# The latent attention of a two-layer trunk: its steps put in a fixed order on three engines, weight conversions at named blocks, and one value tile earlier

## The chip, the cores and the metric

One Trainium2 chip, one of its cores. The time is the device time of one launch in microseconds (us); a kernel's time is the median of several runs. The engines are named PE (matrix products and transposes), DVE (vector), ACT (scalar and activation), POOL (GpSimd) and SP, whose queue issues the transfers from HBM. Each runs its own program in order and waits on semaphores for the others.

## The reference

Two layers of a decoder trunk, 512 positions of width 1024, one sequence, float32. Each layer is feed-forward, token mixer, feed-forward, all with a norm before and after and a modulation (shift, scale, gate) computed from a vector `c`. The mixer of the first layer, which alone is touched here, is latent attention with 16 heads; the second layer's is a dilated window attention.

```python
def mla(h, w_in, q_norm, w_q_up, kv_norm, w_kv_up, w_o):
    lat = h @ w_in
    cq, ckv = lat[..., :384], lat[..., 384:640]
    k_rope = lat[..., 640:][:, :, None, :]
    q = (rmsnorm(cq, q_norm) @ w_q_up).reshape(B, S, 16, 64 + 32)
    kv = (rmsnorm(ckv, kv_norm) @ w_kv_up).reshape(B, S, 16, 64 + 64)
    q = concat([q[..., :64], rope(q[..., 64:], pos)])
    k = concat([kv[..., :64], rope(k_rope, pos) broadcast to the heads])
    v = kv[..., 64:]
    s = q k^T * 96 ** -0.5, causal;  p = softmax(s)   # per head
    return (p v, heads side by side) @ w_o
```

## The kernel before

Six sub-layers run one after the other: feed-forward, latent attention, feed-forward, feed-forward, dilated attention, feed-forward. Every weight is split, after its transfer, into two numbers of a reduced format: `whi` (a rounded copy, on ACT, L132) and `wlo` (what the rounding left, on DVE, L134, in two halves). A product is then three matmuls on PE (L147 to L149). PE is the engine with most to do, and the rest of the program is written to keep it supplied.

Latent attention works feature-major: a tile is 128 features (partitions) by 512 positions. First the latents are projected and normed (`head`, `norm`). The norm's last step, per latent tile and half of the positions, is DVE L773, then a rounded copy on ACT L776 (`hh`), then the rest on DVE L777 (`hl`). Then `rest` takes over. It works on 8 pairs of heads, c = 0 to 7, and for each pair on four groups of 128 query positions, i = 0 to 3. One (c, i) is a block, n = 4c + i, 32 blocks in all. Causality makes the scores of block i 128(i + 1) wide. For each of the two heads of the pair, a block does

- score: one matmul (L879) into a bank of PSUM; on DVE a masked scale with a minimum over the row (L882, called the reduce here), which reads the bank and so sets it free; on ACT the exponential with its sum (L885); then, for both heads at once, a reciprocal on DVE (L888), and the division: head 0 on DVE (L890), head 1 on ACT (L891);
- turn: transposes of the probabilities on PE (L907) into banks of a second kind ("aux"), and copies to SBUF: for i < 2 on DVE (L909), for i of 2 and 3 one head on ACT (L911) and one on DVE (L912). The copies are named `silu` for even and `gg` for odd i;
- weigh: after odd i, the products of the probabilities with the values of blocks i - 1 and i (L928), into one aux bank for the whole pair; after i = 3 `put_o` splits that bank into two parts (ACT L708, DVE L709).

`Pipe(2)` staggers them: in the step that scores a block, PE also turns the block two steps back and weighs an earlier one. Banks: four for scores and projections ("mm", taken in turn), four of the kind "aux". A matmul into a bank waits until what the bank held was read.

Beside the blocks, a table `BESIDE` names for each block which projections are written right behind it: `key(g, p)` (copies on ACT L809, DVE L810, POOL L812), `query(g, p)` (two copies on ACT L819), `value(j, e)` (6 products and a copy on ACT L797), and `rope(g)`. `rope` makes the rotated part of four heads' queries from one product: a shuffle and a multiplication on DVE (L825, L826), one multiplication on POOL (L827), the addition on DVE (L828), then copies: two on ACT (L836), two on POOL (L834). Here g is a group of four heads; `weight(g, 0)` holds its key and rope columns and `weight(g, 1)` its query columns, and each is transferred and converted where it is first called.

Instructions of all engines are ordered by a scheduler, which sees the program in the order in which it is written and moves instructions by its own estimates. So in the kernel before, the order on PE, ACT and DVE in this stretch is the scheduler's. Conversions of the weights, for instance, stand between the steps of the blocks wherever the scheduler put them, one half apart from the other in places.

Of the kernel before, what the change touches and what calls it, by code (L numbers as in the profile page):

```python
# [535 lines left out]
class Ffn:  # L536
# [104 lines left out]

class Pipe:
# [71 lines left out]
class Mla(Mixer):  # L714
# [66 lines left out]
    def project(self, w, at, us):  # L781
# [3 lines left out]
            t.mm3(b, [x[:, at + j, :] for x in w], self.latn[u], j == 0, j == len(us) - 1)  # L785
        return b

    def value(self, j, e):
        t = self.t
        if not self.wv:  # L790
            self.wv += [t.weights(t.a["mla_v"][k], flat=True) for k in range(2)]
        b = t.bank()
        for k in range(2):
            ls = [x[:, j * P : (j + 1) * P] for x in self.latn[k]]
            t.mm3(b, ls, [x[:, e * SEQ : (e + 1) * SEQ] for x in self.wv[k]], k == 0, k == 1)
        self.v[j, e] = t.s()
        t.nc.scalar.activation(self.v[j, e], b, AF.Copy)  # L797
# [23 lines left out]
    def rope(self, g):  # L821
        t, nc = self.t, self.t.nc
        b = self.project(self.weight(g, 0), 4, (3, 4, 5))
        t1, t2 = t.s(), t.s()
        nc.vector.stream_shuffle(t2, b, [(c + 16) % 32 for c in range(32)])  # L825
        nc.vector.tensor_tensor(t1, b, self.cos, ALU.mult)  # L826
        nc.gpsimd.tensor_tensor(t2, t2, self.sin, ALU.mult)  # L827
        nc.vector.tensor_tensor(t1, t1, t2, ALU.add)  # L828
        for p in range(2):
            q = self.q[2 * g + p] = [t.s() for _ in range(2)]  # L830
            for e in range(2):
                r = t1[64 * p + 32 * e : 64 * p + 32 * e + 32]
                if p:
                    nc.gpsimd.tensor_scalar(q[e][64:96], r, 1.0, 0.0, ALU.mult, ALU.add)  # L834
                else:
                    nc.scalar.activation(q[e][64:96], r, AF.Copy)  # L836


    BESIDE = {
        1: (("query", 0, 1),),  # L840
        2: (("value", 3, 0),),
        3: (("key", 1, 0),),
        4: (("rope", 1),),
        5: (("query", 1, 0),),
        6: (("value", 0, 1),),
        8: (("key", 1, 1),),
        9: (("query", 1, 1),),
# [13 lines left out]
        28: (("part", 0),),  # L861
        29: (("part", 1),),
        30: (("part", 2),),
    }

    def attend(self, c, i, pipe):
        t, nc = self.t, self.t.nc
        sc = 96.0**-0.5
        if i == 0:
            self.st = t.tmp.tile([P, 4, 6], F32, tag="st", name="st", bufs=3), {}  # L870
        st, box = self.st
        q, k = self.q[c], self.k[c]

        def score(i):
            n = (i + 1) * P
            box[i] = []
            for e in range(2):
                s = t.bank()[:, :n]
                nc.tensor.matmul(s, q[e][0:96, i * P : n], k[e][0:96, :n], start=True, stop=True)  # L879
                p = (t.t("u", UB) if i % 2 else t.t("sq", SB))[:, :n]  # L880
                nm, z = st[:, i, e : e + 1], st[:, i, 2 + e : 3 + e]
                nc.vector.tensor_tensor_reduce(  # L882
                    p, s, self.mask[:, SEQ - n :], -sc, 3e38, ALU.add, ALU.min, accum_out=nm
                )
                nc.scalar.activation(p, p, AF.Exp, bias=nm, scale=-1.0, accum_out=z)  # L885
                box[i].append(p)
            r = st[:, i, 4:6]
            nc.vector.reciprocal(r, st[:, i, 2:4])  # L888
            p = box[i]
            nc.vector.tensor_scalar(p[0], p[0], r[:, 0:1], None, ALU.mult)  # L890
            nc.scalar.activation(p[1], p[1], AF.Copy, scale=r[:, 1:2])  # L891

        def turn(i):
            n = (i + 1) * P
            tag = "gg" if i % 2 else "silu"
            ps = [t.bank("aux")]
            ys = [t.t(tag)]
            if i < 2:
                ps.append(ps[0][:, n:])
                ys.append(ys[0][:, n:])  # L900
            else:
                ps.append(t.bank("aux"))
                ys.append(t.t(tag))
            for e in range(2):
                for j in range(i + 1):
                    r = slice(j * P, (j + 1) * P)
                    nc.tensor.transpose(ps[e][:, r], box[i][e][:, r], t.ident)  # L907
            if i < 2:
                nc.vector.tensor_copy(ys[0][:, : 2 * n], ps[0][:, : 2 * n])  # L909
            else:  # L910
                nc.scalar.activation(ys[0][:, :n], ps[0][:, :n], AF.Copy)  # L911
                nc.vector.tensor_copy(ys[1][:, :n], ps[1][:, :n])  # L912
            box[i] = ys

        def weigh(i):
            if i == 0:
                box["o"] = t.bank("aux")
            elif i % 2:
                for q in (i - 1, i):
                    products(q)  # L920
            if i == 3:
                self.put_o(box["o"])

# [12 lines left out]

        pipe.push(i, score, turn, weigh)

    def rest(self):
        self.t.gates(self)  # L940
        self.wv, self.wqk, self.v, self.q, self.k = [], {}, {}, {}, {}
        pipe = Pipe(2)
        self.key(0, 0)
        self.value(0, 0)
        self.value(1, 0)
        self.key(0, 1)
        self.t.count(99)
        self.rope(0)
        self.query(0, 0)
        self.value(2, 0)  # L950
        for c in range(8):
            for i in range(4):
                if (c, i) == (7, 0):
                    self.t.new_y()
                self.attend(c, i, pipe)
                for name, *args in self.BESIDE.get(4 * c + i, ()):
                    getattr(self, name)(*args)
        for ns in ((3, 4, 5), (6, 7)):
            pipe.step()
            for n in ns:  # L960
                self.part(n)
        pipe.flush()


class Dil(Mixer):
# [622 lines left out]
```

## Time and profile before

| | |
|---|---|
| median of 3 runs | 2256.52 us (2256.39 to 2257.5) |
| the profiled execution, its own time | 2258.68 us |
| its span, first to last instruction | 2256.5 us |
| mean granted clock of PE | 0.996 of full speed |
| busy: PE, DVE, ACT, POOL | 2217.8, 1183.6, 848.3, 106.3 us |
| latent attention's `rest` | about 436 to 590 us of the span |

Times in the profile count from the span's start. A row of the timeline gives start, length, engine, line, operation, what is written from what, shapes, a count where several are run together, and in brackets the idle time ahead with what ended it. A row of a group gives total busy time and the mean of one in ns, then the engine's idle time before these instructions with the releasers. A row of waits gives who waited for whom: total us, times, the longest.

### The profile page before, as it was taken

What the parts mean: (1) busy time and instruction counts of PE and PEld (TensorE: products, weight loads), DVE (VectorE), ACT (ScalarE), POOL (GpSimd) and SP (SyncE); (2) the same over time, 40 slices, a digit from 0 to 9 for tenths busy, and PEclk for the clock granted to TensorE, in tenths of its full rate; (3) what the DMA queues carried; (4) which work ended last, traced back from release to release, by engine and by line L of the source; (5) the groups of instructions that cost most, each with busy time, mean ns of one, the idle gap of its engine ahead of it and who ended that gap; (6) DMA issues with size and microseconds to landing.
All of it is one profiled execution on the core that took longest, in us unless ns stands there. A gap on an engine that the chain in (4) does not pass through costs nothing. (4 is left out here: it accounts for less than half of the span.)

```text
span 2256.5 us, 30151 instructions
## 1 busy us (share of the span) xinstructions
PE 2217.8 (98%) x11354; PEld 1868.9 (83%) x11354; DVE 1183.6 (52%) x2691; ACT 848.3 (38%) x1730; POOL 106.3 (5%) x143
## 2 busy tenths in 40 slices
PE   7999999999999999999999999999999998999998
PEld 5888888877898888898888889988899878888887
DVE  7666575677665356474464463234424466333344
ACT  4422234577633132352221353434342545322232
POOL 1000001210110000020000010000000002000000
PEclk9999999999999999999999999999999999999999
DMA  8575762311255365334653533334343442233231
GB/s 309 158 245 186 195 219 69 110 52 57 66 167 181 110 187 181 127 121 136 175 179 119 159 117 111 101 103 93 72 114 110 89 129 66 83 120 101 79 112 38
DMA packets 124056, 290.33 MB, mean 129 GB/s; under 512 B 44786, under 2 KB 49157, under 8 KB 123910
## 3 DMA queue, kind: packets, MB, share of 16 engines
q1 hardware_dynamic: 123910, 288.41, 41.6%
q8 instruction: 89, 1.46, 0.3%
q14 instruction: 57, 0.47, 0.1%
HBM read 281.76 MB, written 4.49 MB: 127 GB/s over the span
## 5 line engine op out<-in xcount | busy, mean ns | idle before, releaser
L134 DVE TENSOR_TENSOR wlo<-raw,whi 128x512 fp32r<-128x512 f32 (+1 forms) x714 | 467.4, 692 | 593.8 <-ACT whi L132 592.6
L147 PE MATMUL mm<-s,whi 128*128 128x512 f32 (+1 forms) x1932 | 722.1, 374 | 2.4 <-ACT whi L132 2.4
L149 PE MATMUL mm<-s,wlo 128*128 128x512 f32 (+1 forms) x1932 | 719.2, 372 | 0.0
L148 PE MATMUL mm<-s,whi 128*128 128x512 f32 (+1 forms) x1932 | 719.0, 372 | 0.0
L132 ACT ACTIVATE whi<-raw 128x1024 fp32r<-128x1024 f32 (+1 forms) x357 | 368.8, 1048 | 785.2 <-PE mm L148 531.6
L147 PEld LDWEIGHTS mm<-s,whi 128*128 128x128 f32 x1932 | 364.3, 189 | 69.3 <-issue 3.5
L149 PEld LDWEIGHTS mm<-s,wlo 128*128 128x128 f32 x1932 | 364.6, 189 | 63.5
L148 PEld LDWEIGHTS mm<-s,whi 128*128 128x128 f32 x1932 | 364.6, 189 | 61.7
L147 PE MATMUL mm<-whi,s 128*128 128x512 f32 (+1 forms) x1040 | 407.1, 391 | 4.1 <-ACT s L708 4.1
L149 PE MATMUL mm<-whi,s 128*128 128x512 f32 (+1 forms) x1040 | 404.7, 389 | 1.2 <-DVE s L709 1.2
L148 PE MATMUL mm<-wlo,s 128*128 128x512 f32 (+1 forms) x1040 | 405.2, 390 | 0.0
L147 PEld LDWEIGHTS mm<-whi,s 128*128 128x128 f32 x1040 | 211.2, 203 | 39.7 <-ACT s L708 4.5
L149 PEld LDWEIGHTS mm<-whi,s 128*128 128x128 f32 x1040 | 211.3, 203 | 36.1 <-DVE s L709 1.6
L148 PEld LDWEIGHTS mm<-wlo,s 128*128 128x128 f32 x1040 | 211.3, 203 | 34.0 <-issue 0.3
L169 DVE CUSTOM_DVE_ANT_0 raw<-raw,cs 128x1024 f32<-128x1024 f32 x130 | 159.4, 1232 | 124.4 <-DMA raw<-w_mod 123.9
L463 DVE TENSOR_TENSOR s<-mm,s 128x512 f32<-128x512 f32 x112 | 76.8, 690 | 121.1 <-PE mm L149 121.1
L322 POOL TENSOR_TENSOR mv<-mv,mhalf 128x1 f32<-128x1 f32 x48 | 36.2, 756 | 1493.5 <-DVE mv L321 1491.0
L1092 ACT ACTIVATE s<-mm 128x128 f32<-128x128 f32 (+3 forms) x109 | 33.1, 358 | 163.6 <-PE mm L149 159.7
L586 ACT ACTIVATE s<-gg 128x512 fp32r<-128x512 f32 (+1 forms) x97 | 57.4, 592 | 47.1 <-DVE gg L585 47.1
L585 DVE TENSOR_TENSOR gg<-silu,mm 128x512 f32<-128x512 f32 (+1 forms) x95 | 59.9, 630 | 12.0 <-ACT silu L583 12.0
L1203 ACT ACTIVATE u<-u,y 128x128 f32<-128x128 f32 x128 | 49.6, 397 | 23.8 <-issue 13.1
L583 ACT ACTIVATE silu<-mm 128x512 f32<-128x512 f32 (+1 forms) x95 | 51.4, 541 | 18.3 <-PE mm L149 18.2
(185 smaller groups left out, 1682.7 us busy)
## 6 DMA issues: line engine op xcount, KB each, us to landing
raw<-w_gu SPq DMA_DIRECT2D x168, 512.0 KB, 4.2
raw<-w_mod SPq DMA_DIRECT2D x130, 512.0 KB, 4.6
raw<-w_down SPq DMA_DIRECT2D x88, 512.0 KB, 4.3
raw<-dil_in SPq DMA_DIRECT2D x47, 512.0 KB, 4.1
raw<-dil_v SPq DMA_DIRECT2D x20, 512.0 KB, 3.7
s<-w_mod SPq DMA_DIRECT2D x28, 256.0 KB, 5.7
raw<-w_gu SPq DMA_DIRECT2D x16, 256.0 KB, 3.7
raw<-mla_o SPq DMA_DIRECT2D x8, 512.0 KB, 3.9
```

Of the source, the lines that this page charges most:

```text
L132: self.nc.scalar.activation(hi, raw, AF.Copy)
L134: self.nc.vector.tensor_tensor(lo[:, r], raw[:, r], f(hi[:, r]), ALU.subtract)
L147: mm(out, w[0], m[0], start=first, stop=False)
L148: mm(out, w[0], m[1], start=False, stop=False)
L149: mm(out, w[1], m[0], start=False, stop=last)
L169: nc.vector.tensor_tensor_reduce(raw, raw, self.cs, 1.0, 0.0, ALU.mult, ALU.add, accum_out=t[:, 0:1])
L322: nc.gpsimd.tensor_tensor(v[:, 1:2], v[:, 0:1], self.mhalf[:, 0:1], ALU.pow)
L463: nc.vector.tensor_tensor(y, b, y, ALU.add)
L583: nc.scalar.activation(s, banks[0], AF.Silu)
L585: nc.vector.tensor_tensor(v, s, banks[1], ALU.mult)
L586: nc.scalar.activation(ghi, v, AF.Copy)
L1203: nc.scalar.activation(c, c, AF.Exp, bias=pair["top"][:, g, i, one], scale=-1.0, accum_out=pair["z"][:, g, i, one],)
```

## The change

Nothing is added to what is computed and nothing left out; the same operations are written in another order, and in one stretch the scheduler is told to keep it.

1. The stretch of `rest` from the first key to the last block stands in `manual_schedule` for PE, ACT and DVE: on these three engines its instructions keep the order in which they are written. POOL and SP stay with the scheduler, and so does all else of the program, of which instructions may still be placed between those of the stretch.
2. The first key-and-rope weights, the two value weights and the first query weights are called before that stretch, in this order. For the others a table `AHEAD` names a block behind which they are called, and there stand their conversion's instructions: for group 1 blocks 0 and 2, for group 2 blocks 6 and 7, for group 3 blocks 10 and 11, and the first three out weights (`out_weights`, used by the last blocks' `part`) blocks 18, 22 and 25.
3. `value(3, 0)`, the fourth tile of values, is written ahead of the first scores, and three entries of `BESIDE` move up one block: key(1, 0), rope(1) and query(1, 0) now stand behind blocks 2, 3 and 4.
4. `attend` writes score, turn and weigh of its step first and then the reciprocal and the division of the block it scored (`share`). The splitting of the output (`put_o`) and rope's addition with its copies are put in a list and written at the end of the next step (`follow`).

```diff
-        if not self.wv:
-            self.wv += [t.weights(t.a["mla_v"][k], flat=True) for k in range(2)]
...
-        nc.vector.tensor_tensor(t1, t1, t2, ALU.add)
...
+        def add():
+            nc.vector.tensor_tensor(t1, t1, t2, ALU.add)
...
+        self.behind.append(add)
...
     BESIDE = {
         1: (("query", 0, 1),),
-        2: (("value", 3, 0),),
-        3: (("key", 1, 0),),
-        4: (("rope", 1),),
-        5: (("query", 1, 0),),
+        2: (("key", 1, 0),),
+        3: (("rope", 1),),
+        4: (("query", 1, 0),),
...
+    AHEAD = {
+        0: (("weight", 1, 0),),
+        2: (("weight", 1, 1),),
+        6: (("weight", 2, 0),),
+        7: (("weight", 2, 1),),
+        10: (("weight", 3, 0),),
+        11: (("weight", 3, 1),),
+        18: (("out_weights", 0),),
+        22: (("out_weights", 1),),
+        25: (("out_weights", 2),),
+    }
...
+        def share(i):
             r = st[:, i, 4:6]
             nc.vector.reciprocal(r, st[:, i, 2:4])
...
-                self.put_o(box["o"])
+                self.behind.append(lambda: self.put_o(box["o"]))
...
         pipe.push(i, score, turn, weigh)
+        share(i)
+        self.follow()
+
+    def follow(self):
+        behind, self.behind = self.behind, []
+        for step in behind:
+            step()
...
+        self.weight(0, 0)
+        self.value_weights()
+        self.weight(0, 1)
+        with self.t.tc.manual_schedule(engines={PE, ACT, DVE}):
...
+            self.value(2, 0)
+            self.value(3, 0)
+            for c in range(8):
+                for i in range(4):
+                    n = 4 * c + i
...
+                    self.attend(c, i, pipe)
+                    for name, *args in (*self.BESIDE.get(n, ()), *self.AHEAD.get(n, ())):
+                        getattr(self, name)(*args)
```

How the instructions stand now. SP's and POOL's rows come in the same order as before. The scores' and products' order on PE differs only by item 3's moves. DVE and ACT differ through the whole stretch; three places follow. In these rows `x2` means two alike in a row, and the small ISA row behind a reduce reads its minimum.

DVE at the start of the blocks, before (rope's shuffle, product and addition, the wlo halves of weight(1, 0), the reduces of blocks 0 and 1, then the reciprocal of block 0):

```order
L825 STREAM_SHUFFLE s<-mm 128x512
L826 TENSOR_TENSOR s<-mm,s 128x512
L134 TENSOR_TENSOR wlo<-raw,whi 128x448
L828 TENSOR_TENSOR s<-s 128x512
L134 TENSOR_TENSOR wlo<-raw,whi 128x448
L882 ISA sq,st<-mm,s 128x128
```

and now:

```order
L827 STREAM_SHUFFLE s<-mm 128x512
L828 TENSOR_TENSOR s<-mm,s 128x512
L832 TENSOR_TENSOR s<-s 128x512
L900 ISA sq,st<-mm,s 128x128
L900 ISA st 128x1
L900 ISA sq,st<-mm,s 128x128
L900 ISA st 128x1
L908 RECIPROCAL st<-st 128x2
L910 TENSOR_SCALAR sq<-sq,st 128x128
L134 TENSOR_TENSOR wlo<-raw,whi 128x448 x2
L900 ISA u,st<-mm,s 128x256
```

The two halves of the weights moved from beside rope's addition to behind block 0's reciprocal and division, and ahead of block 1's first reduce; block 0's reciprocal moved ahead of block 1's reduces.

ACT at blocks 3 to 5, before (the copy of block 3's transposed probabilities is the `gg` row, L911):

```order
L891 ACTIVATE u<-u,st 128x512
L911 ACTIVATE silu<-aux 128x384
L885 ACTIVATE sq,st<-sq,st 128x128 x2
L891 ACTIVATE sq<-sq,st 128x128
L911 ACTIVATE gg<-aux 128x512
L885 ACTIVATE u,st<-u,st 128x256
L836 ACTIVATE s<-s 32x512 x2
L885 ACTIVATE u,st<-u,st 128x256
L819 ACTIVATE s<-mm 64x512
```

and now:

```order
L911 ACTIVATE u<-u,st 128x512
L903 ACTIVATE sq,st<-sq,st 128x128 x2
L931 ACTIVATE silu<-aux 128x384
L911 ACTIVATE sq<-sq,st 128x128
L840 ACTIVATE s<-s 32x512 x2
L821 ACTIVATE s<-mm 64x512 x2
L903 ACTIVATE u,st<-u,st 128x256 x2
L931 ACTIVATE gg<-aux 128x512
L911 ACTIVATE u<-u,st 128x256
```

The `gg` copy (now L931) moved behind the two rope copies, the two query copies and block 5's exponentials.

ACT near the end of the blocks, before (L132 converts out weights):

```order
L911 ACTIVATE silu<-aux 128x384
L132 ACTIVATE whi<-raw 128x1024
L885 ACTIVATE sq,st<-sq,st 128x128
L891 ACTIVATE sq<-sq,st 128x128
L819 ACTIVATE s<-mm 64x512 x2
L885 ACTIVATE u,st<-u,st 128x256 x2
L911 ACTIVATE gg<-aux 128x512
L132 ACTIVATE whi<-raw 128x1024
L891 ACTIVATE u<-u,st 128x256
```

and now, at blocks 25 and 26:

```order
L903 ACTIVATE u,st<-u,st 128x256 x2
L931 ACTIVATE gg<-aux 128x512
L911 ACTIVATE u<-u,st 128x256
L132 ACTIVATE whi<-raw 128x1024 x4
L903 ACTIVATE sq,st<-sq,st 128x384 x2
L911 ACTIVATE sq<-sq,st 128x384
```

Four conversions now stand in a row ahead of block 26's exponentials: that of the third out weights, and three of the next ones, which are called behind the stretch.

More of the change, by code (lines that the diff above doesn't have):

```diff
@@ L786, in project, with value_weights @@
         return b
+    def value_weights(self):
+        t = self.t
+        self.wv = [t.weights(t.a["mla_v"][k], flat=True) for k in range(2)]
     def value(self, j, e):
         t = self.t
-        if not self.wv:
-            self.wv += [t.weights(t.a["mla_v"][k], flat=True) for k in range(2)]
         b = t.bank()
@@ L827, in rope @@
         nc.gpsimd.tensor_tensor(t2, t2, self.sin, ALU.mult)
[L828 to L836, printed above, removed]
+        def add():
+            nc.vector.tensor_tensor(t1, t1, t2, ALU.add)
+            for p in range(2):
+                q = self.q[2 * g + p] = [t.s() for _ in range(2)]
+                for e in range(2):
+                    r = t1[64 * p + 32 * e : 64 * p + 32 * e + 32]
+                    if p:
+                        nc.gpsimd.tensor_scalar(q[e][64:96], r, 1.0, 0.0, ALU.mult, ALU.add)
+                    else:
+                        nc.scalar.activation(q[e][64:96], r, AF.Copy)
+        self.behind.append(add)
     BESIDE = {
         1: (("query", 0, 1),),
-        2: (("value", 3, 0),),
-        3: (("key", 1, 0),),
-        4: (("rope", 1),),
-        5: (("query", 1, 0),),
+        2: (("key", 1, 0),),
+        3: (("rope", 1),),
+        4: (("query", 1, 0),),
         6: (("value", 0, 1),),
@@ L941, in rest @@
         self.wv, self.wqk, self.v, self.q, self.k = [], {}, {}, {}, {}
+        self.behind = []
         pipe = Pipe(2)
[L943 to L962, printed above, removed]
+        self.weight(0, 0)
+        self.value_weights()
+        self.weight(0, 1)
+        with self.t.tc.manual_schedule(engines={PE, ACT, DVE}):
+            self.key(0, 0)
+            self.value(0, 0)
+            self.value(1, 0)
+            self.key(0, 1)
+            self.t.count(99)
+            self.rope(0)
+            self.follow()
+            self.query(0, 0)
+            self.value(2, 0)
[3 more added lines that the diff above has]
+                    n = 4 * c + i
+                    if n == 28:
+                        self.t.new_y()
+                    self.attend(c, i, pipe)
+                    for name, *args in (*self.BESIDE.get(n, ()), *self.AHEAD.get(n, ())):
+                        getattr(self, name)(*args)
+            for ns in ((3, 4, 5), (6, 7)):
+                pipe.step()
+                self.follow()
+                for n in ns:
+                    self.part(n)
+            pipe.flush()
+            self.follow()
 class Dil(Mixer):
```

## The prediction

> **What bounds the kernel now.** I read the page first, then the waits of the matrix engine (PE) from 430 to 600 us, the stretch in which the latent attention runs, then stretches of it, then the instructions where it loses time. All else of the program keeps its order.
>
> ```profile
> PE 2217.8 (98%) x11354; PEld 1868.9 (83%) x11354; DVE 1183.6 (52%) x2691; ACT 848.3 (38%) x1730; POOL 106.3 (5%) x143
> ...
> PE mm L879 <- ACT s L819: 0.8, 1, 0.8
> PE mm L879 <- ACT s L836: 0.6, 1, 0.6
> ...
> 448.50:457.00 8.50, 7.08 (x25) 5.34 (x25) 3.28 (x15) 7.25 (x17) 2.69 (x4) 0.80 0.18 63
> 457.00:540.00 83.00, 83.00 (x549) 63.54 (x548) 65.38 (x200) 65.89 (x160) 13.93 (x19) 1.00 0.19 58
> 540.00:570.00 30.00, 29.73 (x194) 21.96 (x195) 19.90 (x62) 21.64 (x55) 0.00 (x0) 1.00 0.11 36
> ...
> 448.60:452.00 3.40, 2.06 (x10) 1.73 (x11) 1.59 (x8) 3.31 (x5) 2.69 (x4) 1.00 0.43 152
> 452.00:455.40 3.40, 3.40 (x10) 2.62 (x9) 0.70 (x4) 2.50 (x11) 0.00 (x0) 0.50 0.01 5
> ```
>
> PE is the bound. In a row of stretches stand the length, the busy time of PE, weight loads, DVE, ACT and POOL, then the granted clock. At the first scores, whose line is L879, PE stands still for 1.42 us (8.50 less 7.08) and waits for ACT; then come 83 us without a gap, and one more gap of 0.27 (30.00 less 29.73). A stretch of 3.4 us at half clock follows the first gap and costs 0.20 x 8.50 = 1.7. All that can be gained here is 1.42 + 0.27 + 1.7 = 3.4 us, 0.15% of 2256.5. A gain over 0.2% (4.5 us), which a measurement could tell from none, isn't there.
>
> But ACT is busy for 65.9 of those 83 us and DVE for 65.4, 79% each, and PE goes through without a wait because their steps stand in an order that has each result ready in time. So a step put ahead of the wrong one soon reaches PE.
>
> ```profile
> 457.25 0.39 PE L149 MATMUL mm<-whi,s 128*128 128x512 f32 x1
> 457.47 0.39 PE L147 MATMUL mm<-whi,s 128*128 128x512 f32 x1
> 474.48 1.88 PE L879 MATMUL mm<-s 96*128 96x512 f32 x4
> 476.20 0.60 PE L907 MATMUL aux<-ident,u 128*128 128x128 f32 x4
> ...
> 446.08 1.28 POOL L827 TENSOR_TENSOR s<-s 128x512 f32<-128x512 f32 x1 [4.99 <-issue]
> 446.42 1.42 DVE L134 TENSOR_TENSOR wlo<-raw,whi 128x448 fp32r<-128x448 f32 x1
> 447.77 0.68 DVE L828 TENSOR_TENSOR s<-s 128x512 f32<-128x512 f32 x1
> 448.37 0.61 DVE L134 TENSOR_TENSOR wlo<-raw,whi 128x448 fp32r<-128x448 f32 x1
> 448.48 1.28 ACT L836 ACTIVATE s<-s 32x512 f32<-32x512 f32 x2 [0.69 <-DVE s L828]
> 449.78 0.59 ACT L819 ACTIVATE s<-mm 64x512 f32<-64x512 f32 x1
> 450.40 0.60 ACT L797 ACTIVATE s<-mm 128x512 f32<-128x512 f32 x1
> 451.01 1.28 ACT L885 ACT_TABLE_LOAD   x1
> 452.31 0.40 ACT L885 ACTIVATE sq<-sq,st 128x128 f32<-128x128 f32 x1
> 540.52 0.47 ACT L911 ACTIVATE silu<-aux 128x384 f32<-128x384 f32 x1
> 540.89 1.05 ACT L132 ACTIVATE whi<-raw 128x1024 fp32r<-128x1024 f32 x1
> ```
>
> A full-width product comes every 0.22 us (457.25 to 457.47), a 512-wide score every 0.43 (four from 474.48 to 476.20). The scores of block 2 are three quarters as wide, two in each, so one head takes some 0.65. An ACT step may start 0.1 before the last ends (540.52 + 0.47 against 540.89), and DVE's 0.08 (446.42 + 1.42 against 447.77). With these and the groups below I add up by hand when each step of the new program order can start, PE, DVE and ACT each strictly in their order: a step starts when its engine is free and what it reads, or the bank it overwrites, is ready. Clocks below are those of this addition.
>
> ```profile
> L134 DVE TENSOR_TENSOR wlo<-raw,whi 128x512 fp32r<-128x512 f32 x18 | 11.7, 684 | 3.9 <-ACT whi L132 3.9
> L882 DVE CUSTOM_DVE_ANT_0 u<-mm,s 128x512 f32<-128x512 f32 x16 | 10.8, 686 | 2.1 <-PE mm L879 1.9
> L885 ACT ACTIVATE sq<-sq,st 128x384 f32<-128x384 f32 x16 | 9.7, 607 | 2.9 <-DVE st L882 2.9
> L882 DVE CUSTOM_DVE_ANT_0 u<-mm,s 128x256 f32<-128x256 f32 x16 | 6.7, 421 | 2.9 <-PE mm L879 2.7
> L885 ACT ACTIVATE u<-u,st 128x256 f32<-128x256 f32 x16 | 8.0, 501 | 0.7 <-DVE st L882 0.5
> L879 PE MATMUL mm<-s 96*128 96x384 f32 x32 | 11.8, 490 | 0.0
> L709 DVE TENSOR_TENSOR s<-aux,s 128x512 fp32r<-128x512 f32 x8 | 5.5, 688 | 2.9 <-ACT s L708 2.8
> L909 DVE COPY gg<-aux 128x512 f32<-128x512 f32 x8 | 5.5, 686 | 0.0
> L888 DVE RECIPROCAL st<-st 128x2 f32<-128x2 f32 x32 | 5.2, 163 | 10.1 <-ACT sq L885 6.6 <-ACT u L885 3.1
> L911 ACT ACTIVATE gg<-aux 128x512 f32<-128x512 f32 x8 | 4.7, 587 | 4.3 <-PE aux L907 4.2
> L890 DVE TENSOR_SCALAR sq<-sq,st 128x384 f32<-128x384 f32 x8 | 3.7, 463 | 0.2
> L891 ACT ACTIVATE sq<-sq,st 128x128 f32<-128x128 f32 x8 | 3.2, 398 | 1.2 <-DVE st L888 1.1
> L169 DVE CUSTOM_DVE_ANT_0 raw<-raw,cs 128x1024 f32<-128x1024 f32 x2 | 2.4, 1222 | 0.0
> L132 ACT ACTIVATE whi<-raw 128x896 fp32r<-128x896 f32 x2 | 1.9, 946 | 1.2 <-PE mm L148 1.2
> ```
>
> **The change part by part.** (Lines are those of before.) No operation is new and none is dropped, so every duration has its row; the unknown is what the order does. No transfer moves: SP's and POOL's rows stay, so asking for weights at a named block moves only L132 on ACT and L134's two halves on DVE.
>
> The start. value(3,0) puts 6 x 0.23 = 1.4 us of products where PE stood. But the third query latent's two halves now come one after another behind L773 and L777, and rope's product waits 0.54 for them. The rope add, freed of the wlo half ahead of it, starts at 448.5, ACT copies both rope parts (1.28), then both query parts (0.59 each). PE, done with value(3,0) at 450.5, waits 0.5 for the first head, 0.3 for the second and 0.1 for a bank. Sum 1.4: what the fourth tile fills is lost to rope and to ACT's order. Nothing is gained.
>
> Block 2. ACT is done with the copies at 451.4, does two value copies (0.5 each with the overlap), the table load (1.28), block 0's two exponentials (0.4 each), and at 454.8, after the reciprocal, the scale (0.4); only then whi of weight(1,0) (0.95), to 456.05. DVE has the two wlo halves next (0.54 each), then block 1's first reduce (0.42 less overlap): 457.6. The second score of block 2 takes the bank that this reduce frees. PE has done the first scores (from 451.5), query(0,1)'s nine products (9 x 0.23 = 2.1) and the first head's score (0.65) and is there at 455.5. Stall 2.2. Behind the waiting score on PE stand block 0's transposes and value products, which nothing else could use the time for; behind the wlo halves on DVE stand both of block 1's reduces, and ACT's exponentials wait for these, so ACT idles 1.7 too. Before, these halves lay ahead of block 0's reduce (446.42, 448.37), beside products.
>
> Block 4, the same with weight(1,1), whose whi comes behind block 2's scale and a key copy, and whose two halves of 384 stand ahead of block 3's reduces: 1.1. PE waits for the bank of block 3's first head.
>
> Block 6. PE wants the copy of block 3's probabilities at 473.56. Before it stood ahead of the rope parts on ACT; now there are two of these, two query copies and two exponentials of 256 ahead, and it ends at 475.2: 1.7. (Two rope parts 1.2, two query copies 1.0, two exponentials 1.0 and the copy 0.6 make 3.8 from 471.4, when the rope add releases ACT.)
>
> Block 8. wlo of weight(2,0) and two 512 reduces (0.62 each) stand ahead of the copy L909 (0.69): 1.6. Block 9, wlo of weight(2,1) ahead of block 8's reduces: 0.9, and 0.45 for the ACT copy that comes late with them. Blocks 13 and 14: the modulation dot L169 (1.2) and wlo of weight(3,1) ahead of a reduce: 1.5, then twice 0.45. Blocks 17 and 20: 0.3 and 0.4. Block 24: the second out weights, named after block 22, have whi on ACT behind L708 and two halves (0.6 each, L134's row) on DVE ahead of block 23's 512 reduce: PE, at 547.4 for the bank, gets it at 549.65, so 2.2, and 0.1 behind it.
>
> Block 28. After block 25 ACT does four L132 of 1024 in a row, 4 x 0.95 = 3.8: the third out weights, named there, and the three next, which stand outside the fixed stretch and which the scheduler puts right behind. Before, single ones stood between copies (540.89). Block 26's exponentials (0.5 each) start at 561.9, the reciprocal runs at 563.5, a wlo half stands ahead of the scale L890, ready at 564.8. PE has wanted it since 561.7, after 0.3 for a bank: 3.1. Late next: L708 and L709 of the output (0.5), and two 512 reduces and L909 (1.6). After block 29 another 0.2 for L909.
>
> Sum of idle: 1.4 + 2.2 + 1.1 + 1.7 + 1.6 + 1.35 + 2.4 + 0.7 + 2.3 + 5.5 + 0.2 = 20.4. Less the 1.7 of before: +18.7. The half-clock stretch followed a gap that is now broken up, so I take off its 1.7: +17.0. The profiled execution's span of 2256.5 is the median's 2256.52; so 2273.5.
>
> These waits grow from small differences. With ACT and DVE steps 5% shorter the sum is +11.5, with 10% +7, with 15% +3.5, with 5% longer +21. The same addition over the order of before gives 1.66 us of idle where the trace has 1.69, but there the slack hides errors of the steps. A step's overlap with the next (0.1 of 0.6) is itself 16%, taken from few rows; 10% shorter to 5% longer is my doubt, and I take the rows as they are.
>
> Half clock came after only 1.34 us of idle within 3.4 (3.40 less 2.06). [...]
>
> **The rivals.** *The new waits are absorbed.* For it: DVE and ACT are idle 21% of the time. Against: the stalls come from order, not load. It decides from steps some 14% shorter than their rows on: there the sum falls under 0.2%, since the copies and reduces reach PE in time nearly everywhere. Wholly absorbed, only the start changes: -1.7 for the clock, and -0.7 of idle if value(3,0) covers half of the 1.42: 2254, no change that can be told.
>
> *Only the conversions ahead of reduces bite* (2.2 + 1.1 + 0.9 + 1.5 + 0.4 + 2.2 = 8.3), ACT's order and the four L132 in a row being covered: about 2264.8. For it: these need no exact hit of two engines. Against: the four L132 are 3.8 us on the path between two blocks.
>
> *The clock falls at the long stalls.* Five places lose over 1.5 us; each may bring 3.4 us at half speed, 1.7, and less where DVE catches up meanwhile: up to 5 x 1.7 = 8.5 more, 2282. For it: the row of 0.50. [...]
>
> *The change speeds the kernel* by a fixed order alone: bounded by the 3.4 us above, so at best 2253, no difference that can be told.
>
> **How the numbers follow.** My sum 0.60, conversions alone 0.18, clock falls 0.13: these are slower, 0.91. Absorbed 0.08 is no change. Faster 0.01. The range goes from 2262, a little under the second case and the 10% end (2256.5 + 7 = 2263.5), to the clock's 2282; what is left out is mostly the absorbed case and the last of the 10% end.
>
> **What would show it.** In the lines of the changed kernel: right if PE's waits name L900 (reduce), L931 and L929 (copies) and L910 (scale), with PE idle near 20 us between 440 and 590; the longest, about 3, where L910 comes behind the out weights. Wrong: PE idle under 5 us there, or idle at the first scores gone and rope's product not waiting. If ACT's or DVE's busy time fell, the steps are cheaper than in these rows and the sum is too high; if the granted clock falls in more than one stretch after 455 us, it is too low.

## The result, and the profile after

The changed kernel takes 2276.05 us (median of 4 runs, 2275.17 to 2277.72), the kernel before 2256.55: a ratio of 1.0089, 95% interval 1.0074 to 1.0104. The profiled execution has a span of 2273.4 us, against 2256.5. The forecast was slower, 2273.5 us.

First the page of the changed kernel, then PE's waits between 430 and 620 us, then the places on PE's timeline where it stood still, then stretches of 3.4 us (columns as before: length, busy time of PE, weight loads, DVE, ACT and POOL, granted clock, share of the transfer engines).

```profile
PE 2224.9 (98%) x11354; PEld 1870.8 (82%) x11354; DVE 1182.3 (52%) x2691; ACT 849.2 (37%) x1730; POOL 105.8 (5%) x143
...
PE mm L897 <- DVE st L900: 6.6, 4, 2.4
PE aux L927 <- DVE sq L910: 2.7, 1, 2.7
PE aux L948 <- DVE gg L929: 2.5, 2, 1.3
PE aux L948 <- ACT gg L931: 1.6, 1, 1.6
PE mm L897 <- ACT s L821: 0.6, 1, 0.6
PE aux L948 <- DVE s L709: 0.3, 1, 0.3
PE aux L927 <- ACT silu L931: 0.2, 1, 0.2
...
458.12 1.23 PE L897 MATMUL mm<-s 96*128 96x384 f32 x2 [2.22 <-DVE st L900]
476.35 1.09 PE L948 MATMUL aux<-gg,s 128*64 128x128 f32 x16 [1.65 <-ACT gg L931]
483.94 0.66 PE L948 MATMUL aux<-gg,s 128*64 128x128 f32 x8 [1.28 <-DVE gg L929]
504.87 0.70 PE L897 MATMUL mm<-s 96*128 96x256 f32 x2 [1.37 <-DVE st L900]
551.52 0.46 PE L897 MATMUL mm<-s 96*128 96x128 f32 x2 [2.37 <-DVE st L900]
566.59 0.85 PE L927 MATMUL aux<-ident,sq 128*128 128x128 f32 x6 [2.67 <-DVE sq L910]
...
458.60:462.00 3.40, 3.40 (x10) 2.50 (x9) 1.81 (x7) 3.16 (x10) 0.00 (x0) 0.50 0.35 116
506.40:509.80 3.40, 3.40 (x11) 2.82 (x10) 2.52 (x6) 0.60 (x2) 0.00 (x0) 0.50 0.54 188
567.90:574.60 6.70, 5.51 (x22) 3.92 (x21) 4.07 (x15) 3.79 (x11) 0.00 (x0) 0.50 0.45 150
```

Before, PE waited in the stretch for ACT's copies at the first scores (1.4 us) and once 0.2 us for a division. Now it waits for reduces (L900), a division (L910) and copies of turned probabilities (L929, L931). The waits come to 14.5 us, the longest is 2.7. From 440 us on, four stretches of 3.4 us run at half clock (the last three rows, granted clock 0.50; the third row is two of them), where there was one.

How long does the attention take? The next feed-forward layer begins with ACT's table load, a fixed point of the program. In the kernel before and then in the changed one:

```profile
619.57 1.28 ACT L583 ACT_TABLE_LOAD   x1
```

```profile
639.62 1.28 ACT L583 ACT_TABLE_LOAD   x1
```

The attention ends 20.05 us later. The span is only 16.9 longer, so 3.2 us come back behind it. PE's longest waits in the second layer show the half of that (before, then the changed kernel):

```profile
1861.51 0.64 PE L147 MATMUL mm<-whi,s 128*128 128x512 f32 x1 [4.13 <-ACT s L708]
```

```profile
1879.88 0.50 PE L147 MATMUL mm<-whi,s 128*128 128x512 f32 x1 [2.40 <-ACT s L708]
```

A wait of 4.13 is now 2.40, and the half-clock stretch that followed it before (1861.7 to 1865.1 at a granted clock of 0.50, some 1.7 us by estimate) is missing: from 1840 to 1920 us the changed kernel's clock is 1.00. Nothing there was changed, and why the wait is shorter was not followed up. It is no lasting gain: in a second profile of the changed kernel, in the last group below, 1.2 us come back instead of 3.2.

### The profile page after: what moved, and what is told of

Its sections match the earlier page's. It is cut to its first block, busy times and chain, and to the rows that moved or that the text cites. A ratio compares the mean times of both kernels' runs of the same rounds, so it can differ in the third digit from the quotient of the medians.

```text
span 2273.4 us, 30134 instructions
## 1 busy us (share of the span) xinstructions
PE 2224.9 (98%) x11354; PEld 1870.8 (82%) x11354; DVE 1182.3 (52%) x2691; ACT 849.2 (37%) x1730; POOL 105.8 (5%) x143
## 5 line engine op out<-in xcount | busy, mean ns | idle before, releaser
L132 ACT ACTIVATE whi<-raw 128x1024 fp32r<-128x1024 f32 (+1 forms) x357 | 368.6, 1048 | 784.2 <-PE mm L148 546.4
```

Source lines behind the costliest of these rows:

```text
L132: self.nc.scalar.activation(hi, raw, AF.Copy)
```

## The experiments

Ten kernels and the changed one a second time ran, in three groups, each beside the kernel before on its own chip; ratios are to that. Each profile gives the idle time of PE from 435.5 to 600 us (164.50 less PE's busy time); in the changed kernel it is 14.8 us, in the one before 1.7. This is the sum of the gaps between PE's rows. It serves to compare kernels; the waits themselves are longer, as the part on the prediction shows.

### Is it the fixed order, and on which engine?

Four kernels have the changed text and fix the order on fewer engines.

**The scheduler orders all three engines again.**

```diff
-        with self.t.tc.manual_schedule(engines={PE, ACT, DVE}):
+        if True:
```

> The changed kernel's text, with the fixed order taken away: the scheduler orders PE, ACT and DVE again. If the loss comes from the order that the written text gives on ACT and DVE (my theory), the scheduler repairs it: adding up the rows over its order gives 0.2 us of PE idle in the attention, so about 2253 to 2255 (no first gap, no half-clock stretch after it). If the loss comes from the text itself (value tile ahead, conversions at named blocks, reciprocal later), the time stays above 2265.

Measured: 2254.9 us beside 2258.65, ratio 0.9986 (0.9977 to 0.9995). In the stretch PE is idle for 0.75 us at full clock, and the next layer starts at 615.73:

```profile
435.50:600.00 164.50, 163.75 (x1000) 127.37 (x1000) 116.08 (x326) 117.51 (x277) 23.60 (x32) 1.00 0.20 60
...
615.73 1.28 ACT L583 ACT_TABLE_LOAD   x1
...
1857.10:1863.80 6.70, 4.73 (x11) 3.77 (x12) 3.76 (x6) 3.01 (x7) 0.00 (x0) 0.50 0.05 21
1880.90:1887.70 6.80, 5.74 (x26) 5.52 (x26) 6.29 (x14) 6.09 (x15) 2.98 (x4) 0.50 0.62 166
```

So the written text is not slow in itself: with the scheduler's order the attention even ends 3.8 us earlier than before (1.3 of it a half-clock stretch at 404 us, ahead of the change, that this execution lacks: ACT's copy L749 that starts at 419.62 us before starts at 418.43 here; how the 1.3 is found stands further down). The span is only 1.7 shorter (2254.8): in this execution the second layer has four half-clock stretches of 3.4 us, two and two (the last two rows, clock 0.50), where the kernel before had one. This version beats both kernels, the one before by 0.14%.

**Fixed on PE alone** (`engines={PE}`).

> Fixed order on PE alone, ACT and DVE by the scheduler. My theory: PE's order is innocent, idle 0.3 us in the attention, about 2253 to 2255. Rival: a fixed order on PE, which can no longer put a ready product ahead of a waiting score, carries the loss: above 2265.

Measured: 2255.58 us, ratio 0.9986 (0.9977 to 0.9995), again 0.75 us of idle. PE's order alone costs nothing. No kernel fixes ACT and DVE with PE left free, so what PE's order adds when all three are fixed is not shown.

**Fixed on PE and DVE** (`engines={PE, DVE}`).

> Fixed order on PE and DVE, ACT by the scheduler. Adding up the rows gives 5.9 us of idle (0.5 at rope, 0.8 at block 2, 0.5 at block 4, 1.4 at block 8, 2.3 at block 28): 2256.5 + 4.2 = 2261 without a half-clock stretch, 2262 to 2264 with one or two. If DVE's order alone carried the loss it would be about 2274; if ACT's alone, 2254.

Measured: 2262.29 us, ratio 1.0020 (1.0011 to 1.0029), idle 4.8 us where 5.9 was forecast. DVE's order alone does not carry the loss (2274), nor does ACT's (2254). The waits are for the same lines, smaller:

```profile
PE aux L948 <- DVE gg L929: 2.4, 2, 1.2
PE mm L897 <- DVE st L900: 1.5, 3, 0.7
PE aux L927 <- DVE sq L910: 0.4, 1, 0.4
```

**Fixed on PE and ACT** (`engines={PE, ACT}`).

> Fixed order on PE and ACT, DVE by the scheduler. By the rows 2.5 us of idle (0.6 at the first scores, 0.7 at block 6, 0.8 at block 8, small ones): 2256.5 + 0.8 = 2257.3 without a half-clock stretch. If the two engines' orders each carried their part of the loss, what DVE's lacked (2276 less the 2262.3 with PE and DVE fixed, some 14 us) would be here: 2270.

Measured: 2260.01 us beside 2257.28, ratio 1.0012 (1.0003 to 1.0021), idle 3.4 us: 2.7 us slower where 0.8 was forecast, not the 13 of the rival. The waits, 1.8 at block 6 and 1.0 at the copies L929:

```profile
PE aux L948 <- ACT gg L931: 1.8, 1, 1.8
PE aux L948 <- DVE gg L929: 1.0, 2, 0.6
```

One engine's fixed order gives 4.8 or 3.4 us of idle, both together 14.8. The same beside the scheduler's order of the same text, whose next layer starts at 615.73: it starts at 621.53 with DVE fixed, 5.8 later; at 620.18 with ACT fixed, 3.2 later if the 1.3 of the stretch at 404 us, which this execution has (L749 at 419.58), are taken off; and at 638.45 with both fixed (the changed kernel in the last group, without that stretch), 22.7 later. So the loss is in the two orders together. The likely reason is that they hand work to and fro (a reduce, an exponential, a reciprocal, a division; a `whi` and then its halves): with one engine free, the scheduler can put its steps so that the other's lateness is met; with both fixed, each waits for the other. That is a reading of the rows, and no run tests it by itself.

### Which steps are in the wrong place?

**The halves of `wlo` at the end of the next block's steps**, fixed order kept.

```diff
+        def low():
+            for r in (slice(0, n // 2), slice(n // 2, n)):
+                self.nc.vector.tensor_tensor(lo[:, r], raw[:, r], f(hi[:, r]), ALU.subtract)
+        self.put_off.append(low) if self.put_off is not None else low()
...
         share(i)
+        lows, t.lows = t.lows, []
+        for low in lows:
+            low()
         self.follow()
...
+                    self.t.put_off = self.t.lows
+                    for name, *args in self.AHEAD.get(n, ()):
+                        getattr(self, name)(*args)
+                    self.t.put_off = None
```

> The changed kernel with one thing moved: the two wlo halves of the weights named in the table stand at the end of the next block's steps on DVE, behind its reduces, copies and division, and no longer ahead of them. Everything else, the fixed order too, stays. Theory: idle falls from 20.4 to about 9.3 us by the rows (block 2's 2.2 becomes 1.4 for the weights themselves, the stalls at blocks 4, 8, 9, 13, 14 and 24 and the 3.1 at block 28 go, 1.8 at block 6 and 1.2 + 1.6 at block 28 stay): 2262 to 2267 with one to three half-clock stretches. Rival (the halves are not what the reduces wait for): 2276 as the changed kernel.

Measured: 2268.14 us beside 2258.65, ratio 1.0041 (1.0027 to 1.0054), idle 7.4 us. Where PE stood longest, and at block 24, and then the conversions on ACT near block 26:

```profile
457.47 0.50 PE L152 MATMUL mm<-s,wlo 128*128 128x512 f32 x1 [1.12 <-DVE wlo L136]
473.69 1.40 PE L951 MATMUL aux<-gg,s 128*64 128x128 f32 x16 [1.99 <-ACT gg L934]
542.63 0.46 PE L900 MATMUL mm<-s 96*128 96x128 f32 x2 [0.39 <-DVE st L903]
556.94 0.44 PE L951 MATMUL aux<-silu,s 128*64 128x128 f32 x4 [1.05 <-DVE s L712]
558.76 0.66 PE L951 MATMUL aux<-gg,s 128*64 128x128 f32 x8 [1.38 <-DVE gg L932]
...
551.59 1.04 ACT L133 ACTIVATE whi<-raw 128x1024 fp32r<-128x1024 f32 x1
...
553.73 1.04 ACT L133 ACTIVATE whi<-raw 128x1024 fp32r<-128x1024 f32 x1
```

The waits at blocks 8, 9 and 13 are out of the list, the 2.37 at block 24 is 0.39 and the 2.67 at block 28 is gone; block 2 waits 1.12 for the weights themselves. That is the forecast's list, place by place. The time lies above the forecast's 2262 to 2267, which were counted from 2256.5; the kernel before took 2258.65 in this group, so 9.5 us of loss are left where there were 19.5.

One thing more moved with the halves. The scheduler places the conversions called behind the stretch, and here it did not put them in a row with the one ahead: one starts at 551.59, one at 553.73 and two at 555.67, with block 26's exponentials and division between them. So block 28, whose waits fell from 4.1 to 2.4 us, is not the halves' alone. The other 5.7 us of the 7.4 that went are theirs, so their place on DVE makes some 40 to 50% of the idle time. The rest is ACT's copy at block 6 and the output part and the copy behind block 28 (L712, L932), and there are two half-clock stretches still (full-width products start 0.43 us apart from 475.62 to 477.32 and from 559.69 to 562.68, elsewhere 0.23; the clock over the 164.50 us is 0.98).

**The next three out weights named behind blocks 28, 29 and 30.**

```diff
         25: (("out_weights", 2),),
+        28: (("out_weights", 3),),
+        29: (("out_weights", 4),),
+        30: (("out_weights", 5),),
```

> The changed kernel with the next three out weights named behind blocks 28, 29 and 30, so that no four conversions stand in a row on ACT. If the four in a row are the cause of the last long stall, its 2.7 us and what follows (1.4) mostly go: 2272. By the rows over the new order the place gains 1.8 but a 3.7 us stall comes at the pair's last weighing, where the DVE copy stands behind two wlo halves that wait for their whi, and some 0.5 elsewhere: about 2278.

Measured: 2279.77 us beside 2256.92, ratio 1.0094 (1.0079 to 1.0110).

```profile
564.71 0.85 PE L930 MATMUL aux<-ident,sq 128*128 128x128 f32 x6 [1.06 <-DVE sq L913]
588.19 0.95 PE L951 MATMUL aux<-gg,s 128*64 128x128 f32 x8 [3.35 <-DVE gg L932]
```

With no four conversions in a row the stall at block 28 falls from 2.67 to 1.06, but a copy on DVE is now late at the last weighing and PE waits 3.35 there. Spreading them over these three blocks was no cure, as forecast (2278); other places for them were not tried.

**ACT's copies ahead of the exponentials.**

```diff
-                nc.scalar.activation(p, p, AF.Exp, bias=nm, scale=-1.0, accum_out=z)
+                exps.append((p, nm, z))
...
+        exps = []
         pipe.push(i, score, turn, weigh)
+        for p, nm, z in exps:
+            nc.scalar.activation(p, p, AF.Exp, bias=nm, scale=-1.0, accum_out=z)
         share(i)
```

> The changed kernel with ACT's exponentials of a block written behind the copies of the block turned in the same step, so that the copy of block 3 no longer waits for block 5's two exponentials. By the rows block 6 gains 1.0 and the stalls for the ACT copy at blocks 9 and 14 (0.45 each) go, but block 8 loses 1.1 more and some 0.5 is lost elsewhere: the sum stays, 2276 within 2. Rival (each stall can be mended by itself): 2274.

Measured: 2278.98 us beside 2256.92, ratio 1.0095 (1.0081 to 1.0108): a little above the 2276 within 2 that was expected, and not told from the changed kernel's ratio.

```profile
473.80 1.09 PE L948 MATMUL aux<-gg,s 128*64 128x128 f32 x16 [0.52 <-ACT gg L931]
483.00 0.66 PE L948 MATMUL aux<-gg,s 128*64 128x128 f32 x8 [2.28 <-DVE gg L929]
```

Block 6's wait falls from 1.65 to 0.52, and block 8's grows from 1.28 to 2.28. Beside the changed kernel in the last group, PE reaches block 8 some 0.7 us earlier (480.72 for 481.38) and DVE's copy comes 0.3 later (483.00 for 482.66), behind a reciprocal that the exponentials put off made late. So most of what block 6 gains is waited away at block 8. Not every stall can be mended by itself.

### The fourth tile of values

**In the kernel before, value(3,0) alone moved ahead of the first scores.**

```diff
         self.value(2, 0)
+        self.value(3, 0)
...
-        2: (("value", 3, 0),),
```

> The kernel before with one part of the change alone: value(3,0) ahead of the first scores, scheduler as before. By the rows the first gap (1.42 us) goes, 0.6 us of idle stay in the attention, and the half-clock stretch of 1.7 has nothing to follow: about 2253.5 to 2254.5. Rival: the first scores wait as long anyway, for what comes behind the tile on ACT: 2256.5.

Measured: 2256.18 us beside 2256.92, ratio 0.9993 (0.9984 to 1.0002): not told from no change end to end, and the expected 2253.5 to 2254.5 was missed. The trace shows what it does in place: no half-clock stretch at the first scores (clock 1.00 over the 164.50 us), 0.72 us of idle, the next layer 2.6 us earlier than before (616.97). Behind that, this execution takes 1.1 us longer than before (2255.1 less 616.97 is 1638.1, beside 1637.0), and its mean granted clock over the whole span is 0.995 beside 0.996.

```profile
PE mm L878 <- ACT s L819: 0.3, 1, 0.3
...
435.50:600.00 164.50, 163.78 (x997) 127.28 (x997) 115.34 (x324) 117.57 (x277) 22.71 (x31) 1.00 0.20 61
```

**In the changed kernel, value(3,0) back behind block 2.**

```diff
-            self.value(3, 0)
...
-        2: (("key", 1, 0),),
+        2: (("value", 3, 0), ("key", 1, 0)),
```

> The changed kernel with value(3,0) put back behind block 2, all else as changed. By the rows the first gap grows from 1.4 to 2.7 and blocks 2 and 4 lose 0.4 and 0.9 less: the sum is the same, 2276 within 2. If the fourth tile ahead were worth its 1.4 us here, the time would be 2277.5; if the tile ahead were what delays ACT, 2272 or less.

Measured: 2276.35 us beside 2256.92, ratio 1.0085 (1.0071 to 1.0099), the changed kernel's within the interval.

```profile
449.80 1.97 PE L897 MATMUL mm<-s 96*128 96x128 f32 x8 [1.93 <-ACT s L821]
456.25 0.91 PE L897 MATMUL mm<-s 96*128 96x384 f32 x2 [1.77 <-DVE st L900]
```

The first gap is 1.93 in place of 0.57, and the gap after it is 0.45 shorter, with the rest given back later: at block 4, PE waits 0.37 us here, and 1.34 with the tile ahead in the filled kernel below. What the tile fills in one gap is waited for in the next ones.

### What the half-clock stretches cost

**Idle products put where PE waited longest**, and the changed kernel again beside it. The products' results are overwritten by the scores.

```diff
                 s = t.bank()[:, :n]
+                for _ in range({8: 9, 52: 5, 96: 9, 113: 11}.get(4 * (4 * c + i) + e, 0)):
+                    nc.tensor.matmul(s[:, :P], t.ident, t.ident, start=True, stop=True)
                 nc.tensor.matmul(s, q[e][0:96, ...
```

> The changed kernel with idle products (identity by identity, into a bank that the next score overwrites) put on PE where it stood still longest: 9 ahead of block 2's first score, 5 ahead of block 13's, 9 ahead of block 24's, 11 ahead of block 28's second, 0.22 us each, so 7.5 us of idle become work and nothing waits longer. The half-clock stretches behind these four places should go. If the attention is paced by DVE and ACT (my theory), PE at half speed lost only time in which it would have waited at the next place, and the time stays within 1.5 us of the changed kernel's, while stalls that the changed kernel did not show (block 4, 1.1 us) come up. Rival: the four stretches cost 1.7 us each beside the stalls, so 5 to 7 us less than the changed kernel.

> The changed kernel again, beside the filled one on the same chip: 2276 to 2278, 0.85 to 0.95% above the kernel before.

Measured: the filled kernel 2275.93 us, ratio 1.0080 (1.0067 to 1.0092); the changed one 2279.38, 1.0098 (1.0085 to 1.0111), both beside 2257.28. The second is a little above the 2276 to 2278 that was expected. The intervals overlap. The traces say more; first the filled kernel, then the changed one of this group:

```profile
404.56 0.48 DVE L773 SCALAR_TENSOR_TENSOR u<-s,small,aux 128x256 f32<-128x256 f32 x1 [0.97 <-PE aux L278]
636.12 1.28 ACT L583 ACT_TABLE_LOAD   x1
...
435.50:640.00 204.50, 194.00 (x1203) 152.07 (x1203) 135.28 (x364) 135.91 (x312) 28.00 (x38) 1.00 0.18 58
...
465.18 0.46 PE L899 MATMUL mm<-s 96*128 96x128 f32 x2 [1.34 <-DVE st L902]
```

```profile
404.49 0.48 DVE L773 SCALAR_TENSOR_TENSOR u<-s,small,aux 128x256 f32<-128x256 f32 x1 [0.97 <-PE aux L278]
638.45 1.28 ACT L583 ACT_TABLE_LOAD   x1
...
435.50:640.00 204.50, 189.01 (x1114) 146.42 (x1113) 132.95 (x360) 134.42 (x308) 27.25 (x37) 0.97 0.17 54
```

From the norm's step to the next layer it is 231.56 us in the filled kernel and 233.96 in the other. With all four half-clock stretches gone (clock 1.00 for 0.97) the attention is 2.4 us shorter in these two executions. At each of the four places PE still waits 0.20 to 0.36 us behind the idle products, so these held nothing up. In the stretch at 506.4 of the changed kernel's first profile full-width products start some 0.43 us apart (507.34, 507.77, 508.19) and behind it 0.22 (509.86, 510.08), so by estimate 3.4 us hold 1.7 us of work and four stretches take 6.8: some 4.4 were then lost only where PE would have waited at the next place. The wait at block 4, foretold as 1.1 and absent from the changed kernel's trace, is there in the filled one with 1.34. The expectation (within 1.5 us) was too narrow, its rival (5 to 7) too dear.

## Why the prediction was right, and where it was off

The bound on the gain, 3.4 us, held: the best that any kernel gave in the attention is 3.8 us less with the scheduler's order, 2.5 without the stretch at 404, and 0.14% end to end.

That the order, and no transfer, sets the time held: no wait of PE in the stretch is for a transfer, and no conversion on ACT (L132) waited for one. With it the places held: PE waited for L900 at block 2 (2.22, forecast 2.2) and block 24 (2.37, forecast 2.2), for L931 at block 6 (1.65, forecast 1.7), for L929 at block 8 (1.28, forecast 1.6), and longest for L910 behind the four conversions (2.67, forecast 3.1). DVE's rows of the changed kernel at block 2 show the steps that were added up:

```profile
455.29 0.29 DVE L910 TENSOR_SCALAR sq<-sq,st 128x128 f32<-128x128 f32 x1
456.56 1.16 DVE L134 TENSOR_TENSOR wlo<-raw,whi 128x448 fp32r<-128x448 f32 x2 [0.99 <-ACT whi L132]
457.64 0.42 DVE L900 CUSTOM_DVE_ANT_0 u<-mm,s 128x256 f32<-128x256 f32 x1
```

and at block 28 the four conversions on ACT with the division late behind them on DVE:

```profile
559.99 3.88 ACT L132 ACTIVATE whi<-raw 128x1024 fp32r<-128x1024 f32 x4
...
566.03 0.41 DVE L910 TENSOR_SCALAR sq<-sq,st 128x384 f32<-128x384 f32 x1
```

The sum of idle held too, better than the gaps show: these come to 14.8 us, the sum to 20.4. A product's row is 0.39 us long where the next one follows after 0.22, so a gap leaves out some 0.17 of each wait, and all of a shorter one. At rope's product the changed kernel's rows start at 444.14, 444.64 and 445.10, each some 0.25 late, with a gap of 0.10: together the 0.5 that the sum had there. The table gives the gaps of the changed kernel, and how late PE's products start in the filled kernel, which has no half-clock stretch in the attention. That is counted against the kernel with PE's order fixed alone, whose products come in the same order, and at the first scores and block 6, where that kernel waits too, against the usual distance of two products; time filled with idle products is counted in.

| place, times in us | forecast | gaps, changed kernel | late starts, filled kernel |
|---|---|---|---|
| rope and first scores | 1.4 | 0.8 | 1.5 |
| block 2 | 2.2 | 2.2 | 2.4 |
| block 4 | 1.1 | 0 | 1.5 |
| block 6 | 1.7 | 1.7 | 1.9 |
| block 8 | 1.6 | 1.3 | 1.5 |
| block 9 | 1.35 | 0.8 | 1.1 |
| blocks 13 and 14 | 2.4 | 1.5 | 2.4 |
| blocks 17 and 20 | 0.7 | 0 | 1.0 |
| block 24 | 2.3 | 2.4 | 2.5 |
| block 28 | 5.5 | 4.1 | 5.0 |

The forecast's column, with 0.2 behind block 29, comes to 20.4, the last to 20.8. In the changed kernel block 4 and blocks 17 and 20 show no gap: they stand behind half-clock stretches, and PE came later there. "Nothing is gained" at the start held as well: PE's gap at the first scores shrank from 1.42 to 0.70 us, but rope's product took the rest, and putting the tile back changed the total by nothing that can be told.

Three steps were off. In the profiled span their errors cancelled, and that the span came within 0.1 us of the forecast (2273.4 for 2273.5) is luck; the median, 2276.05, is 2.5 above it.

- *"So I take off its 1.7."* That no new stall would bring the clock down, as the sum had it, no run shows: four stretches at half speed came where the sum had none (granted clock 0.50 at 458.6, 506.4 and twice from 567.9), and by the prediction's own sign the sum was then too low. The rival "the clock falls at the long stalls" was right that it falls behind stalls (of 2.22, 1.37 and 2.67 us), and in its places in part: stretches came behind blocks 2 and 28, two of the five places it counted, and behind block 13, and none behind blocks 6, 8 and 24. Its price of 1.7 each was wrong as an addition to the stalls: the filled kernel puts it at 2.4 for all four. As a check on the sum and this price, take the attention as a whole at full clock: the filled kernel's 231.56 us is 16.4 more than the 215.15 of before (404.42 to 619.57). The kernel before had two half-clock stretches there: at 404.2, which is not in the sum and is missing in the filled kernel (L749 at 418.45 there, at 419.62 before), and at 452.0, whose 1.7 the sum took off. Giving 1.3 us back for the first (the first scores come at 451.19 in the changed kernel, which has it, and at 449.89 in the same kernel of the last group, which has not), the attention is 17.7 longer at full clock. The sum said 17.0.
- *"All else of the program keeps its order"*, and by that its time. It does keep its order, yet from the next layer's table load to the end it takes 1637.0 us in the profile of before (2256.5 less 619.57), 1633.8 in the changed kernel's, 1635.8 in the changed kernel's of the last group and 1639.1 in the filled one, with granted clocks of 0.98, 1.00, 0.96 and 0.91 from 1840 to 1920 us (before: 1830 to 1910), by estimate one, no, two and four half-clock stretches of 3.4 us there. The sum had no such term. The span of 2273.4 is 2256.5 with +17.0 as forecast, +2.4 for the clock, +0.7 of size and -3.2 behind the attention, and this last was the execution's.
- *"The profiled execution's span of 2256.5 is the median's 2256.52."* They agree by chance: a span is not a time, and that execution's own time was 2258.68, 2.2 above its span and 2.1 above the median. By the medians the change costs 19.5 us (16.7 to 23.5 by the interval), and 22.1 in the last group. The terms without the last, 17.0 + 2.4 + 0.7 = 20.1, fit that.

Of the rivals, "absorbed" is out, since the four kernels with the order fixed on fewer engines show waits that come and go with it. "Only the conversions ahead of reduces" has about half of the loss: PE's waits for reduces are 6.6 of the 14.8 us, and moving the halves took the idle time to 7.4, of which 1.7 is at block 28, where ACT's order moved too.

## What to carry to other kernels

When an order written by hand takes the place of a scheduler's, add up the engines' rows along the new order before running it: a step put ahead of one that frees a bank can be waited for by the engine that is the bound, though the engine that does the step is idle a fifth of the time (DVE was busy for 65.4 of 83 us before; with two halves of `wlo` ahead of a reduce, PE waited 2.37 us at block 24, and 0.39 with the halves put off). Fixing the order on the bound engine alone cost nothing here (2255.58 beside 2254.9 us), so the helpers can be left to the scheduler. If a helper's order must be fixed, let its steps that free something go first: that took half of this loss away, not all. And look at more than one helper at a time: here two orders that each made the attention 3 to 6 us longer with the other engine free made it 23 us longer together.

## What the runs showed of the hardware

In the traces of the kernel before and of the changed one, the half-clock stretches lie on one grid each. Before, they start at 404.2, 452.0, 1861.7 and 2254.2 us, the later three 14, 427 and 542 times 3.413 us behind the first; in the changed kernel at 404.0, 458.7, 506.4, 567.9 and 2271.1, the later ones 16, 30, 48 and 547 times 3.413 behind the first. Cutting these two executions into windows of that length, with the stretches' starts as edges, and adding up PE's idle time in each gives this count (windows at full clock behind 100 us, without the last two of each execution):

| PE idle in the window of 3.413 us | next window at half clock |
|---|---|
| under 0.5 us | 0 of 1224 |
| 0.5 to 0.9 us | 0 of 9 |
| 0.9 to 1.8 us | 4 of 17 |
| 1.8 to 2.2 us | 0 of 2 |
| 2.2 us and more | 3 of 3 |

A wait of 2.4 us did not always bring a stretch: the 2.37 us at block 24 of the changed kernel lay across two of these windows (1.66 and 0.72 us idle) and brought none. In the kernel with value(3,0) put back, PE waited 2.35 us at the same place, up to 550.34, and products behind it start 0.43 us apart from 553.35 to 554.63, and 0.23 from 555.02 on. That the grid cut the wait in two in the one and not in the other is the likely reason, an estimate from these counts.

```profile
547.40:550.80 3.40, 1.74 (x10) 1.29 (x8) 2.30 (x5) 2.01 (x3) 0.00 (x0) 1.00 0.00 0
455.20:458.60 3.40, 1.18 (x5) 0.43 (x4) 2.19 (x8) 1.68 (x4) 0.00 (x0) 1.00 0.00 0
```

The first of these windows of the changed kernel (1.66 us idle) was followed by full clock, the second (2.22) by the half-clock stretch at 458.6. Why single windows with 0.9 to 1.8 us of idle do bring a stretch, as the 1.34 us before the first scores did, stays open.
